# Encoder layer with retrieval FFN on one core: u blocks between the attention heads, unsplit first-pattern scores, and higher gather rates in the mixing and the up tiles

## The chip, the cores and the metric

The kernel runs on one core of a Trainium2 chip. The metric is the device time of one execution in microseconds (us), lower is better. The engines are named as in the profile: PE (TensorE; PEld is its weight load), DVE (VectorE), ACT (ScalarE), POOL (GpSimd), SP (SyncE, which issues the plain transfers).

## The reference, cut to what matters

One layer of an encoder with 512 tokens of width 1024, then a final norm.

```
h = rmsnorm(x); proj = h @ w_in            # u, v, q (3 patterns x 8 heads x 64), k, v, two gates
y_a = gelu(u) * spatial_gate(rmsnorm(gelu(v)))
y_b = softmax-merge over 3 patterns of banded ALiBi attention(q, k, v)
x = x + (sigmoid(ga) * (y_a @ wa) + sigmoid(gb) * (y_b @ wb)) @ wo
h = rmsnorm(x)
q = h @ w_q                                # 8 heads, two halves of 128
s = q . sub_keys; 16 best of each half; 16 best of the 256 sums -> 128 experts a token
a = gelu(u_tab[expert] . h) * softmax(best)
x = x + sum over experts of a * v_tab[expert]
out = rmsnorm(x)
```

The tables u_tab and v_tab hold 16,384 rows of 1024 floats each.

## The kernel before

**Tokens.** The 512 tokens are four tiles of 128, one for each residue modulo 4. Tile 0 goes ahead alone ("phase A": attention, gating, merge, residual, scores and routing in plain fp32). Tiles 1 to 3 follow together as a group of 384 columns ("phase B"), with fp32 operands split into a high and a low half of type fp32r (helper `split`: ACT makes the high half, DVE the low one) and three matmuls a product in `mm` (L114 to L116). Weights stream through `stream`: SP loads a block of 128 x 1024 floats (512 KB, tile `raw`, four buffers), the block is split into `whi` and `wlo` (two buffers each), and PE uses it. One such block is called a weight pair here, since it holds two slices of the contraction.

**Two ways through the experts.** Tiles 1 and 2 take the dense way: for each of 128 expert blocks an up tile `pu_t` (gelu(u h)) is multiplied by a gate matrix that is built from one-hot rows (`hot`, L760, in `gates`; matmul `pg`; kept in DRAM as `g_dram`, read back as `gl`), and 128 v tiles are accumulated in `acc`. The first 28 pairs of up tiles, 56 in all, are made ahead of the main loop in fp32 (`early`, L112); the other 72 in the main loop with split operands. Tiles 0 and 3 take the sparse way: each of their 128 experts a token is fetched by an indirect transfer of 128 rows, 512 KB, on POOL's queue (L239, `row_of`; eight buffers).

**Gather steps.** The sparse work is a generator, `all_steps`, of 517 steps. For tile 0: 128 u rows, each a dot product on DVE (L261), then 128 v rows in 32 groups of four. A group is eight PE matmuls of 32 columns into `acc_A` (L290): four rows by two halves, written as four different column blocks of the array one after the other, and each of them shows as two records in a trace. Then for tile 3: four routing steps on scores that come back from DRAM, its index tile `eidx` (L329), 128 u rows on DVE (L261) and 128 v rows, each a multiply-add on DVE (`xg`, L338). `gather_steps(us, behind)` is called behind each weight split (WUS), each attention head (HUS), each early up tile (PUS) and each tile of the main loop; it adds `us * rate` to what is owed and takes that many steps. The rate is MIX (0.55) from the attention to the scores of phase B, ATT (0.45) for heads, PRE (0.38) in the early up tiles, and in the main loop whatever spreads the steps that are left. The steps of a place are ordered behind the instructions named there; beyond that the tile scheduler puts the instructions of each engine in an order when the program is built, and each engine runs its own list in that order.

**Places that the change touches.** `attention` projects q in three blocks and runs four pairs of heads behind them; scores of the first pattern are split (`khl`, `q1`), those of the other two are plain fp32. `gating` then projects u in two blocks of four weight pairs, multiplies by the gate `z`, and splits the result into `yaT`. `merge`, `residual` and `scores` follow ("the mixing" below is everything from the merge to the scores of phase B).

## Time and profile before

| what | us |
|---|---|
| median of three runs (1831.03 to 1840.84) | 1839.69 |
| the profiled execution, its own time | 1839.34 |
| its span, first to last instruction | 1837.5 |
| PE busy | 1660.7 (90%) |
| DVE busy | 1324.8 (72%) |
| ACT busy | 715.3 (39%) |
| POOL busy | 696.7 (38%) |
| mean granted TensorE clock, share of full speed | 0.952 |

The transfers moved 548.5 MB, 299 GB/s over the span. A busy share over the whole span mixes stages with different limits, so the stages have to be read one by one. The profiled execution lies within 0.4 us of the median.

### The profile page before, as it was taken

The page shows a single profiled execution, that of the slowest core. Times are in us where ns is not written, and L with a number is a line of the kernel's source. Part 1 is how long each engine was busy: PE and PEld are TensorE (multiplying, and loading weights), DVE is VectorE, ACT ScalarE, POOL GpSimd, SP SyncE. Part 2 cuts the span into 40 slices and gives each one's busy share as a digit, 9 for nine tenths or more (in the row PEclk, how much of TensorE's full clock was granted, in tenths as well). Part 3 has the DMA queues.
Part 4 walks back from the last instruction along what each step waited for, and adds up shares of the span by engine and source line. Part 5 has one row for each costly group of instructions (what it writes and reads, how often), then busy time and mean ns, then how long its engine had stood idle before and what let it go on. Part 6 is the DMA issues. An engine that isn't in the chain of part 4 may idle for free.

```text
span 1837.5 us, 25573 instructions
## 1 busy us (share of the span) xinstructions
PE 1660.7 (90%) x9184; PEld 1390.9 (76%) x9184; DVE 1324.8 (72%) x2818; ACT 715.3 (39%) x1264; POOL 696.7 (38%) x535
## 2 busy tenths in 40 slices
PE   7999887999789999899999976687999999999997
PEld 6988866877589664787778965465768888878886
DVE  3332119899999233488976986598898998988896
ACT  4324211354433212233777830233444444444443
POOL 0000000378774443234431025465554554544440
PEclk9999998998799999899999997988999999999999
DMA  5234875599898888777787589999999999999994
GB/s 194 92 114 153 271 262 188 194 359 356 297 331 320 302 308 282 263 290 281 275 304 265 211 329 403 378 374 362 338 382 351 368 399 358 394 361 364 362 354 150
DMA packets 164335, 548.53 MB, mean 299 GB/s; under 512 B 17008, under 2 KB 37488, under 8 KB 163056
## 3 DMA queue, kind: packets, MB, share of 16 engines
q1 hardware_dynamic: 90480, 278.43, 42.5%
q0 software_dynamic: 73728, 268.47, 39.0%
q8 instruction: 72, 1.18, 0.2%
q14 instruction: 55, 0.45, 0.1%
HBM read 522.19 MB, written 24.64 MB: 298 GB/s over the span
## 4 chain that ended last, share of the span: by engine, by line
PE 61%; DVE 18%; DMA 10%; issue 6%; ACT 3%; POOL 1%; SPq 0%; DVEq 0%; POOLq 0%; ACTq 0%
PE pj L112 6%; PE pj L114 6%; PE pj L116 6%; PE pj L115 6%; PE acc L115 5%; PE pu_t L112 5%; PE acc L116 5%; DVE row L261 4%; PE acc L114 4%; PE acc_A L290 4%; PE pu_t L116 2%; DMA gl<-g_dram 2%; PE pu_t L114 2%; PE pu_t L115 2%; DVE vl L90 2%
## 5 line engine op out<-in xcount | busy, mean ns | idle before, releaser
L239 POOL DMA_INDIRECT row<-in_u_dram,eidx x256 | 363.1, 1418 | 298.5 <-DVE eidx L270 92.0
L261 DVE SCALAR_TENSOR_TENSOR row<-row,h2g 128x1024 f32<-128x1024 f32 x256 | 307.8, 1218 | 12.8 <-DMA row<-in_u_dram,eidx 12.7
L239 POOL DMA_INDIRECT row<-in_v_dram,eidx x128 | 182.0, 1422 | 182.8 <-DVE row L261 86.5
L239 POOL DMA_INDIRECT row<-in_v_dram,eT x128 | 141.7, 1107 | 250.3 <-PE acc_A L290 201.5
L112 PE MATMUL pu_t<-h2T,raw 128*128 128x256 f32 x896 | 209.5, 390 | 28.8 <-DMA raw<-in_ut_dram 28.8
L115 PE MATMUL acc<-vl,ah 128*128 128x512 f32 x512 | 207.2, 416 | 29.0 <-DVE vl L90 28.8
L90 DVE TENSOR_TENSOR wlo<-raw,whi 128x1024 fp32r<-128x1024 f32 x88 | 107.5, 1222 | 155.7 <-ACT whi L89 154.4
L112 PEld LDWEIGHTS pu_t<-h2T,raw 128*128 128x128 f32 x896 | 171.6, 196 | 62.7 <-issue 36.9
L114 PE MATMUL acc<-vh,ah 128*128 128x512 f32 x512 | 194.0, 412 | 17.4 <-ACT vh L89 13.0
L116 PE MATMUL acc<-vh,al 128*128 128x512 f32 x512 | 199.5, 408 | 0.0
L89 ACT CAST whi<-raw 128x1024 fp32r<-128x1024 f32 x88 | 92.3, 1048 | 267.6 <-PE pj L115 177.7
L90 DVE TENSOR_TENSOR vl<-raw,vh 128x1024 fp32r<-128x1024 f32 x128 | 156.1, 1222 | 32.0 <-ACT vh L89 31.9
L114 PE MATMUL pu_t<-h2S_hi,uhi 128*128 128x256 f32 x576 | 164.9, 286 | 6.1 <-ACT uhi L89 5.0
L116 PE MATMUL pu_t<-h2S_hi,ulo 128*128 128x256 f32 x576 | 164.5, 286 | 2.3 <-DVE ulo L90 2.3
L115 PE MATMUL pu_t<-h2S_lo,uhi 128*128 128x256 f32 x576 | 164.4, 285 | 0.0
L338 DVE SCALAR_TENSOR_TENSOR xg<-row,act,xg 128x1024 f32<-128x1024 f32 x128 | 163.9, 1281 | 0.4
L151 POOL TENSOR_TENSOR rs<-ms,mhalf 128x1 f32<-128x1 f32 x16 | 9.0, 563 | 400.5 <-DVE ms L149 302.0
L115 PEld LDWEIGHTS acc<-vl,ah 128*128 128x128 f32 x512 | 100.5, 196 | 65.6 <-DVE vl L90 44.5
L89 ACT CAST vh<-raw 128x1024 fp32r<-128x1024 f32 x128 | 133.0, 1044 | 24.2 <-DMA raw<-in_v_dram 20.1
L114 PEld LDWEIGHTS acc<-vh,ah 128*128 128x128 f32 x512 | 97.6, 197 | 45.3 <-ACT vh L89 19.4
L116 PE MATMUL pj<-hT_hi,wlo 128*128 128x384 f32 (+1 forms) x320 | 103.3, 359 | 18.7 <-DVE wlo L90 18.7
L114 PEld LDWEIGHTS pu_t<-h2S_hi,uhi 128*128 128x128 f32 x576 | 111.5, 194 | 10.8 <-ACT uhi L89 7.2
(238 smaller groups left out, 3426.3 us busy)
## 6 DMA issues: line engine op xcount, KB each, us to landing
raw<-in_ut_dram SPq DMA_DIRECT2D x128, 512.0 KB, 7.0
raw<-in_v_dram SPq DMA_DIRECT2D x128, 512.0 KB, 6.4
raw<-in_w_in_dram SPq DMA_DIRECT2D x88, 512.0 KB, 4.3
raw<-in_wq_dram SPq DMA_DIRECT2D x32, 512.0 KB, 4.5
g_dram<-stg SPq DMA_DIRECT2D x8, 2048.0 KB, 7.4
gl<-g_dram SPq DMA_DIRECT2D x32, 512.0 KB, 8.8
raw<-in_wa_dram SPq DMA_DIRECT2D x16, 512.0 KB, 5.6
raw<-in_wo_dram SPq DMA_DIRECT2D x16, 512.0 KB, 4.8
```

The costliest lines, as they stand in the source:

```text
L89: nc.scalar.copy(hi, src)
L90: return nc.vector.tensor_tensor(lo, src, hi.bitcast(F32), ALU.subtract)
L112: on_pe = nc.tensor.matmul(ps, l[0], r[0], start=first, stop=last)
L114: nc.tensor.matmul(ps, l[0], r[0], start=first, stop=False)
L115: nc.tensor.matmul(ps, l[0], r[1], start=False, stop=False)
L116: on_pe = nc.tensor.matmul(ps, l[1], r[0], start=False, stop=last)
L151: nc.gpsimd.tensor_tensor(rs, ms, mhalf, ALU.pow)
L239: nc.gpsimd.indirect_dma_start(out=row, out_offset=None, in_=table, in_offset=bass.IndirectOffsetOnAxis(ap=at, axis=0))
L261: nc.vector.scalar_tensor_tensor(row, row, 1.0, h2g, op0=ALU.mult, op1=ALU.mult, accum_out=ab[:, k:k + 1])
L290: nc.tensor.matmul(ps[32 * j:32 * j + 32, c], ex[:, j, :], rows[j][:, c], start=n == 0, stop=n == 31)
L338: nc.vector.scalar_tensor_tensor(xg, row, act[:, k:k + 1], xg, op0=ALU.mult, op1=ALU.add)
```

## The change

- The first pattern's scores are one plain fp32 matmul on `kk` and `q`; the split copies `khl` of k and the split of q go away, and k is copied out of PSUM by ACT instead of DVE.
- In phase B the two u blocks of `gating` are projected between the heads of the attention (hook `between`), kept in fp32 in `yaF`, and split into `yaT` after the attention.
- The first q projection of phase B gets a higher scheduling priority.
- Rates: a head takes 4.5 x 0.50 = 2.25 steps (2.03 before), a weight pair of the attention and of the u blocks 4.2 x 0.50 = 2.10 (2.31), a weight pair of the mixing 4.2 x 0.70 = 2.94 (2.31), an early up tile 4.5 x 0.45 = 2.03 (1.71).

```diff
--- before.py
+++ after.py
@@ -40,9 +40,9 @@
 GB = 16
 RB = 4
 GPB = 8
-MIX = 0.55
-ATT = 0.45
-PRE = 0.38
+ATT = 0.5
+MIX = 0.7
+PRE = 0.45
 WUS = 4.2
 HUS = 4.5
 PUS = 4.5
@@ -117,7 +117,7 @@
 
     steps = iter(())
 
-    rate = MIX
+    rate = ATT
     owed = 0.0
     taken = 0
 
@@ -419,7 +419,6 @@
         qsc = kv.tile([P, 4], F32, name="qsc")
         nc.sync.dma_start(qsc, a["qsc"])
         kk = kv.tile([P, 4, 512], F32, name="kk")
-        khl = Op(kv, [P, 4, 512], "khl", False)
         v_sb = kv.tile([P, NR, 512], F32, name="v_sb")
         z = zc.tile([P, NR, D], F32, name="z")
 
@@ -449,8 +448,7 @@
                 nc.vector.scalar_tensor_tensor(z[:, n, :], z[:, n, :], rs, gsgu, op0=ALU.mult, op1=ALU.mult)
 
             def ev_k(b, ps):
-                nc.vector.tensor_copy(kk[:, b, :], ps)
-                khl.put((slice(None), b), kk[:, b, :])
+                nc.scalar.copy(kk[:, b, :], ps)
 
             def ev_v(r, ps):
                 nc.scalar.copy(v_sb[:, r, :], ps)
@@ -465,7 +463,7 @@
                                         sgb[:, g, :].unsqueeze(1).to_broadcast([P, NR, P]), ALU.add)
 
 
-        def attention(pl, cl, x, ybT, exact, hook):
+        def attention(pl, cl, x, ybT, exact, hook, between=None):
             n = len(cl) * P
             bias = pl.tile([P, len(cl), 768], F32, name="bias", bufs=1)
             nc.sync.dma_start(bias, a["abias"][:, cl[0]:cl[-1] + 1, :])
@@ -473,11 +471,11 @@
 
             def q_of(hp):
                 if qs[hp] is None:
-                    qs[hp] = (Op(pl, [P, n], "q1", False), pl.tile([P, 2, n], F32, tag="q2", name="q2"))
+                    qs[hp] = pl.tile([P, 3, n], F32, tag="q", name="q")
                 return qs[hp]
 
             def heads(hp):
-                q1, q2 = q_of(hp)
+                q = q_of(hp)
                 po = pv.tile([P, 512], F32, tag="pv", name="po")
                 for j, r in enumerate(cl):
                     tok = slice(j * P, j * P + P)
@@ -486,9 +484,9 @@
                         slope = 2.0 ** -(head + 1)
                         rows = slice(64 * hh, 64 * hh + 64)
                         s = pst.tile([P, 1024], F32, tag="s", name="s")
-                        mm(s[:, 0:512], q1[rows, tok], khl[rows, hp, :], True, True)
+                        nc.tensor.matmul(s[:, 0:512], q[rows, 0, tok], kk[rows, hp, :], start=True, stop=True)
                         for g in range(2):
-                            nc.tensor.matmul(s[:, 512 + 128 * g:640 + 128 * g], q2[rows, g, tok],
+                            nc.tensor.matmul(s[:, 512 + 128 * g:640 + 128 * g], q[rows, 1 + g, tok],
                                              kk[rows, hp, r * P:(r + 1) * P], start=True, stop=True)
                         pr = pl.tile([P, 768], F32, tag="pr", name="pr", bufs=3)
                         mx = sp.tile([P, 1], F32, tag="mx", name="mx")
@@ -505,7 +503,7 @@
                             last = nc.vector.tensor_tensor(own, own, pr[:, 512 + 128 * g:640 + 128 * g], ALU.add)
                         nc.scalar.activation(pr[:, 0:512], pr[:, 0:512], AF.Copy, scale=rd)
                         if hook:
-                            gather_steps(HUS * ATT / MIX, last)
+                            gather_steps(HUS, last)
                         t = transpose4([pr[:, i * P:(i + 1) * P] for i in range(4)])
                         pt = pl.tile([P, 4, P], F32, tag="pt", name="pt")
                         nc.scalar.copy(pt, t)
@@ -517,32 +515,29 @@
             for j in range(3):
                 def ev_q(b, ps):
                     hp, g = divmod(4 * j + b, 3)
-                    q1, q2 = q_of(hp)
-                    sc = qsc[:, hp:hp + 1]
-                    if g:
-                        nc.scalar.activation(q2[:, g - 1, :], ps, AF.Copy, scale=sc)
-                    else:
-                        nc.scalar.activation(q1.t[0], ps, AF.Copy, scale=sc)
-                        nc.vector.scalar_tensor_tensor(q1.t[1], ps, sc, q1.t[0].bitcast(F32),
-                                                       op0=ALU.mult, op1=ALU.subtract)
-
-                proj_T(a["w_in"][4 + j], KT, x, n, ev_q, exact, hook)
+                    nc.scalar.activation(q_of(hp)[:, g, :], ps, AF.Copy, scale=qsc[:, hp:hp + 1])
+
+                with tc.high_priority(offset=0 if j or not hook else 250):
+                    proj_T(a["w_in"][4 + j], KT, x, n, ev_q, exact, hook)
                 heads(j)
+                if between:
+                    between(j)
             heads(3)
 
-        def gating(pl, cl, x, yaT, exact, hook):
+        def gating(pl, cl, x, put, c, exact, hook):
             n = len(cl) * P
-            for c in range(2):
-                def ev_u(b, ps):
-                    g = 4 * c + b
-                    u = pl.tile([P, n], F32, tag="u", name="u", bufs=3)
-                    nc.scalar.activation(u, ps, AF.Gelu)
-                    u4 = u.rearrange("p (r m n) -> p r n m", r=len(cl), n=NR)
-                    for j, r in enumerate(cl):
-                        nc.vector.tensor_tensor(u4[:, j], u4[:, j], z[:, :, g * P + 32 * r:g * P + 32 * r + 32], ALU.mult)
-                    yaT.put((slice(None), g), u)
-
-                proj_T(a["w_in"][7 + c], KT, x, n, ev_u, exact, hook)
+
+            def ev_u(b, ps):
+                g = 4 * c + b
+                u = pl.tile([P, n], F32, tag="u", name="u", bufs=3) if pl else yaF[:, g, :]
+                nc.scalar.activation(u, ps, AF.Gelu)
+                u4 = u.rearrange("p (r m n) -> p r n m", r=len(cl), n=NR)
+                for j, r in enumerate(cl):
+                    nc.vector.tensor_tensor(u4[:, j], u4[:, j], z[:, :, g * P + 32 * r:g * P + 32 * r + 32], ALU.mult)
+                if put:
+                    put(g, u)
+
+            proj_T(a["w_in"][7 + c], KT, x, n, ev_u, exact, hook)
 
         def merge(pl, cl, x, yaT, ybT, mT, exact, hook):
             n = len(cl) * P
@@ -611,7 +606,8 @@
             with ExitStack() as gq:
                 attention(pool(gq, "qA", 2), [0], lambda kt: hA[:, kt, :], ybT, True, 0)
             m_ = pool(ga, "mA", 1, reuse_waits="tile")
-            gating(m_, [0], lambda kt: hA[:, kt, :], yaT, True, 0)
+            for c in range(2):
+                gating(m_, [0], lambda kt: hA[:, kt, :], lambda g, u: yaT.put((slice(None), g), u), c, True, 0)
             mT = Op(ya_, [P, KT, P], "mA", True)
             merge(m_, [0], lambda kt: hA[:, kt, :], yaT, ybT, mT, True, 0)
             h2A = Op(ya_, [P, KT, P], "h2A", True)
@@ -645,15 +641,23 @@
         py = ExitStack()
         y_ = pool(py, "yB", side="right", reuse_waits="tile")
         ybT = Op(y_, [P, 4, NG], "ybB", False)
+        yaF = y_.tile([P, KT, NG], F32, name="yaF")
         with ExitStack() as gq:
-            attention(pool(gq, "qB", 2, reuse_waits="tile"), GROUP, hB, ybT, False, WUS)
+            qb = pool(gq, "qB", 2, reuse_waits="tile")
+
+            def ev_block(c):
+                if c < 2:
+                    gating(None, GROUP, hB, None, c, False, WUS)
+
+            attention(qb, GROUP, hB, ybT, False, WUS, ev_block)
         pat.close()
+        rate = MIX
         pva = ExitStack()
         acc_A.append(pool(pva, "pva", 1, side="right", space=PSUM, reuse_waits="tile").tile([P, D], F32, name="acc_A"))
         yaT = Op(pool(py, "yaB", side="right", reuse_waits="tile"), [P, KT, NG], "yaB", False)
-        with pz:
-            with ExitStack() as gu:
-                gating(pool(gu, "uB", reuse_waits="tile"), GROUP, hB, yaT, False, WUS)
+        pz.close()
+        for g in range(KT):
+            yaT.put((slice(None), g), yaF[:, g, :])
         pk.close()
         with ExitStack() as gm:
             mT = Op(pool(gm, "mTB", reuse_waits="tile"), [P, KT, NG], "mB", False)
```

The scheduler's order moves with it. The first place is PE in the scores of phase B: `pj` are the products of the scores' projection, `ps` the scores of one block, `acc_A` the matmuls of tile 0's v rows; the number behind x counts matmuls in a row. Before:

```order
L116 MATMUL pj<-h2B_hi,wlo 128x384
L290 MATMUL acc_A<-row,ex 32x512 x8
L603 MATMUL ps<-skc,qT 128x128 x12
L114 MATMUL pj<-h2B_hi,whi 128x384
L115 MATMUL pj<-h2B_lo,whi 128x384
L116 MATMUL pj<-h2B_hi,wlo 128x384
L114 MATMUL pj<-h2B_hi,whi 128x384
```

After the change, at the same place:

```order
L290 MATMUL acc_A<-row,ex 32x512
L114 MATMUL pj<-h2B_hi,whi 128x384
L115 MATMUL pj<-h2B_lo,whi 128x384
L116 MATMUL pj<-h2B_hi,wlo 128x384
L114 MATMUL pj<-h2B_hi,whi 128x384
L115 MATMUL pj<-h2B_lo,whi 128x384
L116 MATMUL pj<-h2B_hi,wlo 128x384
L290 MATMUL acc_A<-row,ex 32x512 x6
L598 MATMUL ps<-skc,qT 128x128 x9
L290 MATMUL acc_A<-row,ex 32x512
L598 MATMUL ps<-skc,qT 128x128 x3
```

The eight matmuls of a group stood together here before; now a group comes as five and three single ones with `pj` or `ps` between them. Over the whole mixing PE's list has 160 matmuls of `acc_A` in 42 runs before (10 of them of eight, 9 of five, 17 of one) and 192 in 89 runs now (20 of five, 65 of one).

The second place is DVE where the early up tiles give way to the main loop: `eidx` are the indices of tile 3, `row,ab` its u rows, `hot` the one-hot rows of the dense gates, `pre` the early up tiles that are multiplied by the gates. Before, from `eidx` on:

```order
L90 TENSOR_TENSOR h2S_lo<-h2T,h2S_hi 128x2048
L329 CAST eidx<-ef_g 128x128
L234 SCALAR_TENSOR_TENSOR o<-xg,rs,gfin 128x512 x2
L841 TENSOR_TENSOR pre<-pre,gl 128x256 x8
L90 TENSOR_TENSOR al<-pre,ah 128x256 x2
L841 TENSOR_TENSOR pre<-pre,gl 128x256 x8
L261 SCALAR_TENSOR_TENSOR row,ab<-row,h2g 128x1024 x6
L841 TENSOR_TENSOR pre<-pre,gl 128x256 x8
L261 SCALAR_TENSOR_TENSOR row,ab<-row,h2g 128x1024
L841 TENSOR_TENSOR pre<-pre,gl 128x256 x8
L261 SCALAR_TENSOR_TENSOR row,ab<-row,h2g 128x1024 x7
L841 TENSOR_TENSOR pre<-pre,gl 128x256 x8
```

After the change:

```order
L234 SCALAR_TENSOR_TENSOR o<-xg,rs,gfin 128x512 x2
L329 CAST eidx<-ef_g 128x128
L764 TENSOR_TENSOR hot<-iota,tt 128x1024 x4
L261 SCALAR_TENSOR_TENSOR row,ab<-row,h2g 128x1024 x3
L764 TENSOR_TENSOR hot<-iota,tt 128x1024 x2
L261 SCALAR_TENSOR_TENSOR row,ab<-row,h2g 128x1024 x3
L764 TENSOR_TENSOR hot<-iota,tt 128x1024 x2
L261 SCALAR_TENSOR_TENSOR row,ab<-row,h2g 128x1024 x4
L764 TENSOR_TENSOR hot<-iota,tt 128x1024 x2
```

All 64 `hot` stood ahead of `eidx` before. Now the last 32 stand behind it and take turns with the u rows of tile 3.

The third place is PE in the early up tiles (`pu_t`, eight matmuls a tile) behind the transposes `tr` for the second token tile's gates, with `pg` for the one-hot matmuls. Before:

```order
L750 MATMUL tr<-ident,ijf 128x128 x2
L750 MATMUL tr<-ident,g_5541 128x128
L112 MATMUL pu_t<-h2T,raw 128x256 x4
L290 MATMUL acc_A<-row,ex 32x512 x8
L112 MATMUL pu_t<-h2T,raw 128x256 x8
L768 MATMUL pg<-hot 128x128 x8
L112 MATMUL pu_t<-h2T,raw 128x256 x9
L768 MATMUL pg<-hot 128x128 x8
```

After the change:

```order
L754 MATMUL tr<-ident,ijf 128x128 x2
L112 MATMUL pu_t<-h2T,raw 128x256 x10
L754 MATMUL tr<-ident,g_5540 128x128
L112 MATMUL pu_t<-h2T,raw 128x256 x13
L772 MATMUL pg<-hot 128x128 x8
L112 MATMUL pu_t<-h2T,raw 128x256 x9
L772 MATMUL pg<-hot 128x128 x8
```

The rows of `acc_A` are no longer in this stretch, since the last group now stands ahead of it (12 early up tiles are behind PE when the last group comes, 25 before). The first eight `pg` of the second token tile, which need the first of the 32 `hot` that moved, stand behind 26 early up tiles.

## Rows read from the trace of the kernel before

**Rows 1.** The page, part 1: busy us (share of the span), instructions.

```profile
PE 1660.7 (90%) x9184; PEld 1390.9 (76%) x9184; DVE 1324.8 (72%) x2818; ACT 715.3 (39%) x1264; POOL 696.7 (38%) x535
```

**Rows 2.** Windows, stage by stage, all engines.

```profile
core 0: us, PE busy (x) PEld busy (x) DVE busy (x) ACT busy (x) POOL busy (x), PEclk, DMA share, GB/s
354.00:590.00 236.00, 208.16 (x1081) 183.66 (x1080) 226.87 (x462) 99.69 (x157) 175.45 (x125) 0.88 0.93 342
590.00:842.00 252.00, 241.89 (x1294) 175.95 (x1294) 115.41 (x314) 67.47 (x96) 94.78 (x91) 0.98 0.80 286
842.00:1079.00 237.00, 237.00 (x1404) 194.28 (x1403) 204.72 (x728) 166.34 (x383) 49.16 (x41) 1.00 0.72 261
1079.00:1169.00 90.00, 56.81 (x213) 45.10 (x213) 48.51 (x101) 6.78 (x18) 41.56 (x35) 0.85 1.04 404
1169.00:1376.00 207.00, 176.96 (x666) 132.01 (x665) 187.67 (x249) 77.77 (x115) 121.48 (x82) 0.92 0.97 363
1376.00:1826.00 450.00, 425.28 (x2603) 375.79 (x2602) 394.37 (x507) 195.39 (x298) 203.18 (x141) 0.98 0.94 353
```

**Rows 3.** Timeline of DVE at the stage ends (start us, us, instruction).

```profile
590.12 0.28 DVE L275 TENSOR_TENSOR act<-act,gate 128x128 f32<-128x128 f32 x1
...
1079.24 0.22 DVE L329 CAST eidx<-ef_g 128x128 int32<-128x128 f32 x1
...
1169.19 1.22 DVE L90 TENSOR_TENSOR vl<-raw,vh 128x1024 fp32r<-128x1024 f32 x1 [16.32 <-ACT vh L89]
...
1374.57 1.21 DVE L90 TENSOR_TENSOR vl<-raw,vh 128x1024 fp32r<-128x1024 f32 x1
1375.71 1.21 DVE L90 TENSOR_TENSOR ulo<-raw,uhi 128x1024 fp32r<-128x1024 f32 x1
```

**Rows 4.** The chain that ended last, 842 to 874 us (start us, us).

```profile
842.34 3.46 PE pu_t L112 x16
845.80 1.85 PE acc_A L290 x16
...
871.71 1.78 PE pg L768 x16
```

**Rows 5.** Windows, the matmuls of `acc_A` alone (line L290).

```profile
590.00:842.00 252.00, 61.66 (x320) 11.19 (x320) 0.98 0.80 286
842.00:1079.00 237.00, 28.08 (x192) 5.69 (x192) 1.00 0.72 261
```

**Rows 6.** Timeline of PE in the merge: a short and a whole run.

```profile
630.34 0.34 PE L115 MATMUL pj<-hT_lo,whi 128*128 128x384 f32 x1
630.61 1.05 PE L290 MATMUL acc_A<-row,ex 128*32 128x512 f32 x2
631.58 0.44 PE L116 MATMUL pj<-hT_hi,wlo 128*128 128x384 f32 x1
631.86 0.34 PE L114 MATMUL pj<-hT_hi,whi 128*128 128x384 f32 x1
632.04 0.33 PE L115 MATMUL pj<-hT_lo,whi 128*128 128x384 f32 x1
...
662.33 1.93 PE L290 MATMUL acc_A<-row,ex 128*32 128x512 f32 x16
664.18 0.44 PE L114 MATMUL pj<-ybB_hi,whi 128*128 128x384 f32 x1
```

**Rows 7.** Windows, `hot` alone (line L760).

```profile
842.00:1079.00 237.00, 74.99 (x64) 1.00 0.72 261
```

**Rows 8.** Timeline of PE in the main loop.

```profile
1405.65 0.40 PE L114 MATMUL acc<-vh,ah 128*128 128x512 f32 x1
1405.88 0.40 PE L115 MATMUL acc<-vl,ah 128*128 128x512 f32 x1
...
1406.35 0.28 PE L114 MATMUL pu_t<-h2S_hi,uhi 128*128 128x256 f32 x1
1406.47 0.28 PE L115 MATMUL pu_t<-h2S_lo,uhi 128*128 128x256 f32 x1
```

## The prediction

> **What bounds the kernel now.** I read the windows first, cut where the work changes hands [rows 2]; the cuts come from the timeline of DVE [rows 3] and from the chain that ended last [rows 4]. Read in each row which engine leaves no time over.
>
> From 354 to 590 us (attention and u blocks of phase B, with tile 0's u rows) DVE is busy for 226.9 of 236 us: DVE is the bound. From 590 to 842 (the mixing) PE is busy for 241.9 of 252 and DVE for less than half: PE is the bound, and what is added to PE's list there is paid in full. From 842 to 1079 (56 early up tiles) PE shows 237 of 237, but what ends the stretch is DVE, which has 204.7 us of routing and `hot` in its list ahead of `eidx`, and about 32 us of waits; until `eidx` is there, no row of tile 3 can be fetched, and transfers fill only 0.72 of their time. From 1079 to 1169 PE, DVE and ACT all have room, and the transfers stand at a share of 1.04 and 404 GB/s: transfers are the bound. From 1169 to 1376 (v tiles alone) DVE has 187.7 of 207 and transfers a share of 0.97: these two share the bound. From 1376 to 1826 (up and v tiles) all three are close: PE 425, DVE 394, transfers 0.94 of 450. The page's 90% for PE [rows 1] hides all this.
>
> **What the change does, in order of time.** The prices come from one execution, and the sum is made against it: its own time is 1839.34 us, span 1837.5, which is the median of the runs shown within 0.4 us.
>
> *Ahead of 354 us.* The split of k and of tile 0's q goes away, k's copy goes to ACT, and eight unsplit scores come in. An fp32 up tile of 256 columns takes 3.46 us for 16 records [rows 4], 0.22 a record and two records a matmul, so 512 columns are about 0.86 us; three split matmuls of 512 columns stand 0.23 apart [rows 8], 0.70 together. So a head costs 0.16 us more on PE, 1.3 us for tile 0's eight heads, and some of it is hidden. I take 0, bounds -5 and +3.
>
> *To 590 us.* In phase B the same 0.16 us for 24 heads is 4 us on PE, which has 28 us to spare in this stretch, so it is hidden behind DVE; if DVE were not the bound it would cost these 4 us. The u blocks bring PE work into a stretch that has room for it, but no DVE work goes away by moving: by DVE's list up to the last u row, three more weight splits stand ahead of it (1.14 us each, the distance of two operations in [rows 3]), eight small operations of the merge come with them, and four splits of q are gone. That is about +5 us, against 9 us of DVE's idle time that better filled lists may win back. I take +3, bounds -6 and +5: the last u row at 593.
>
> *The mixing, now 252 us.* The three weight pairs done early come off PE: 24 matmuls at 0.18 us [rows 6] each, 4.3 a pair, -13. Now the v rows of tile 0. By rates, 24 groups fall here instead of 20. But the price of a group hangs on how its eight matmuls stand. A whole run of eight (16 records) takes 1.85 us [rows 4, 6], so its matmuls, of four column blocks, overlap; a single matmul (2 records) takes 0.97 us, because it has nothing beside it, and on both sides the neighbouring products stand 0.27 and 0.28 apart instead of 0.18, so that it costs 1.16 us in all; a whole run costs 2.03 with the same 0.19 for its neighbours. The order shows 17 single matmuls and 25 longer runs before, 65 and 24 now. With longer runs at the price of a whole one that is 17 x 1.16 + 25 x 2.03 = 70 us before (61.7 busy [rows 5], and 42 x 0.19 for the neighbours: 70), and 65 x 1.16 + 24 x 2.03 = 124 now: +54 us on the engine that is the bound. Lower bound: the mean price of a group before, 70 / 20 = 3.5, for four groups more, +14; upper bound +58, with the shorter runs of before at less. I take 54, since the list of PE is fixed and the rows are of the same kind. The mixing is then 252 - 13 + 54 = 293 us and ends at 886. Transfers have room for 16 more rows here (0.80).
>
> *The early up tiles to `eidx`, now 237 us.* Half of the `hot` now stand behind `eidx`: 32 x 1.17 us [rows 7] = -37. Of DVE's 32 us of waits I take back 19, as an estimate: the last v rows of tile 0 now end with the 12th early tile instead of the 25th, but no row here says how many of the waits hang on them; bounds 0 and 28. That leaves 181 us: `eidx` at 1067, 12 us sooner than now. PE will not fill this stretch any more: 26 up tiles at 3.46 are 90 us, 128 `pg` of two records at 0.11 [rows 4] are 28, and the v rows left, 64 matmuls in 13 single and 10 longer runs, 35; so it comes to the first `pg` that needs a moved `hot` at about 1039 and waits there for some 30 us. This wait is new. Behind it in PE's list stand 30 early up tiles, behind those SP's loads (four `raw` buffers), so the loads of 26 up tiles are left undone in a time when transfers have room.
>
> *From `eidx` to the first v tile, now 90 us at 404 GB/s, 36 MB.* Into this stretch the change pulls: 75 rows of tile 3 that stand in DVE's list ahead of the first v tile (31 before), with eight more in the buffers 43.5 MB at 512 KB each; 26 up tiles, 13.6 MB; the four gate blocks of the second token tile, written at 2.1 MB each, 8.4; 14 loads of `gl`, 7.3; spilled up tiles, `x1` and the first v tiles, 6. Together 79 MB; at 404 GB/s that is 196 us. DVE alone has some 147 us of work for it (32 `hot`, 75 rows, 40 small products), and PE 30 up tiles and 128 `pg`, 132 us. I take 196, since the nearest row is a stretch with the same kinds of transfers; bounds 147 and, at the 363 GB/s of the next stage, 218. The first v tile comes at 1263.
>
> The Trainium skill, "DMA: Bandwidth & Descriptors", section Specifications, gives about 358 GB/s as a core's limit from HBM. The trace disagrees with 404 GB/s over 90 us; by the page's figure the stretch would be 221 us and the time 25 us above mine, and I hold to the row.
>
> *v tiles alone, now 207 us.* 71 rows instead of 82 stand among the 56 tiles in DVE's list: -11 x 1.14 = -13, 194 us, to 1457.
>
> *Up and v tiles, now 450 us.* 110 rows instead of 147: DVE loses 42 us of work and the transfers 19 MB, so both fall clear of the bound. PE's own work is 72 x (24 x 0.12 + 12 x 0.23) = 406 us [rows 8]. I take 418, bounds 406 and 450. This is the change's gain, 32 us; the end of the loop is at 1875. The tail of 11.5 us and the 1.8 us around the span stay: **1889 us**.
>
> So 48 rows leave the last two stages and give 45 us back there; but 44 of them are moved no further than to the stretch behind `eidx`, which the transfers bound and which grows by 106, while the stretch ahead of it gives 56; and the mixing pays 41 for the broken runs less the pairs done early. Sum: 3 + 41 - 56 + 106 - 13 - 32 = +49.
>
> **Rivals.** *No change (1843 us):* the single matmuls cost no more than a group did, +8 us for four whole runs instead of +54. For it: the runs of before are broken too, and PE held. Against it: the pieces stand in the trace with 0.97 us each, and PE had 10 us free in 252. Chance 0.12.
>
> *Faster (about 1798 us):* the rows between the `hot` are hidden, because the stretch from the end of the mixing to the first v tile is paced by PE and not by `eidx` and transfers. PE's work there is 56 x 3.46 for the up tiles, 57 for 256 `pg` and 35 for the v rows left, 286 us; then the first v tile is at 886 + 286 = 1172, 91 us sooner than I have it. For it: transfers have room up to `eidx` (0.72). Against: rows can't be fetched ahead of `eidx`, and 79 MB have to pass behind it. It wins where this stretch takes no more than its present 327 us; I have 377. Chance 0.16.
>
> *Slower still (1911 to 1921 us):* either the transfers behind `eidx` move at 363 GB/s, +22, or the last stage stays at 450 us, +32, because PE waits for v and up tiles and not for rows. For it: in the last stage 44 us of PE's time over its own work are not put down to rows alone by any view. Against: with 37 rows fewer, both DVE and transfers have 10% to spare. Chance 0.14.
>
> **How the numbers follow.** My forecast, 1889 us and 1855 to 1910 by its own bounds, has a chance of 0.58. Within 0.5% (1830 to 1849, about what a measurement can tell from no change) lies the first rival with a little of the forecast's lower edge, 0.13; faster by more is the second rival, 0.16; slower is the rest, 0.71. The range reaches down to the first rival and up to the last one: 1843 to 1921. Left out are the faster case and a few of the rest.
>
> **What would show it.** The mixing of the changed kernel takes some 293 us, and `acc_A` (L290) is busy there for about 110 us with 384 records. `eidx` comes near 1067 and PE has a hole of about 30 us ahead of it. From there to the first v tile the transfers stand at a share near 1 for 190 us or more. In the last stage PE is busy for 97% and the transfers for 0.88. If the mixing takes 250 to 260 us, the step on broken runs is wrong; if the first v tile is there within 327 us of the mixing's end, the step on transfers behind `eidx` is wrong, and the kernel is faster or unchanged; if the last stage keeps 450 us, the rows were not what bound it.

## The result and the profile after

The changed kernel takes 1906.76 us (median of 4 runs, 1903.46 to 1909.41) against 1836.74 us for the kernel before in the same comparison: a ratio of 1.0383, 95% interval 1.0346 to 1.0419, so 3.8% slower. The forecast was 1889 us, range 1843 to 1921. The profiled execution has a span of 1904.4 us and is the one read here.

The page's busy line of the changed kernel, to be held against [rows 1]:

```profile
PE 1709.7 (90%) x9152; PEld 1376.1 (72%) x9152; DVE 1321.2 (69%) x2802; ACT 718.5 (38%) x1267; POOL 709.2 (37%) x535
```

DVE has no more work than before, and the bytes are the same 548.5 MB; PE has 49 us more with 32 instructions fewer. More time in fewer instructions is the first sign that something got dearer, not more.

The windows by stage of the changed kernel, cut at the same events as [rows 2]:

```profile
356.00:606.00 250.00, 226.55 (x1147) 191.65 (x1145) 233.24 (x468) 105.84 (x167) 169.38 (x124) 0.88 0.91 328
606.00:898.00 292.00, 282.99 (x1270) 163.54 (x1270) 111.14 (x315) 62.83 (x89) 109.48 (x104) 0.99 0.76 262
898.00:1079.00 181.00, 147.66 (x780) 107.58 (x778) 165.20 (x687) 88.90 (x199) 29.93 (x29) 0.91 0.58 211
1079.00:1275.00 196.00, 154.16 (x771) 132.86 (x771) 143.40 (x201) 83.98 (x200) 115.42 (x81) 0.90 1.00 387
1275.00:1470.00 195.00, 167.59 (x663) 124.95 (x662) 174.94 (x234) 76.85 (x113) 109.86 (x74) 0.95 0.97 372
1470.00:1893.00 423.00, 414.26 (x2607) 372.15 (x2605) 352.56 (x453) 196.62 (x298) 163.99 (x104) 1.00 0.90 330
```

Stage by stage: the attention 250 us (236 before), the mixing 292 (252), the early up tiles 181 (237), the stretch behind the indices 196 (90), the v tiles alone 195 (207), the last stage 423 (450). The second stage has fewer matmuls than before (1270 records for 1294) and takes 41 us more of PE.

The windows of the matmuls of `acc_A` alone, on PE, in the mixing and in the early up tiles ([rows 5] before: 61.66 us and 28.08 us):

```profile
606.00:898.00 292.00, 115.19 (x384) 0.99 0.76 262
898.00:1079.00 181.00, 31.11 (x131) 0.91 0.58 211
```

Over both stages the work is the same 256 matmuls, and it costs 146 us instead of 90. Why is seen in PE's timeline of the changed kernel, in the merge:

```profile
642.13 0.33 PE L116 MATMUL pj<-yaB_hi,wlo 128*128 128x384 f32 x1
642.39 1.05 PE L290 MATMUL acc_A<-row,ex 128*32 128x512 f32 x2
643.37 0.44 PE L114 MATMUL pj<-yaB_hi,whi 128*128 128x384 f32 x1
643.65 0.34 PE L115 MATMUL pj<-yaB_lo,whi 128*128 128x384 f32 x1
...
649.25 1.90 PE L290 MATMUL acc_A<-row,ex 128*32 128x512 f32 x10
651.08 0.44 PE L116 MATMUL pj<-yaB_hi,wlo 128*128 128x384 f32 x1
```

A single matmul holds PE for 0.98 us (642.39 to 643.37). Five in a row hold it for 1.83 us (649.25 to 651.08), as long as all eight do [rows 6]. So a group that comes as five and three single ones pays for the five what the whole group would cost, and then three times nearly 1 us more.

Waits in PE's timeline and in the table of waits belong to the later stages. In the early up tiles, from PE's timeline:

```profile
1039.55 0.38 PE L754 MATMUL tr<-ident,ijf 128*128 128x128 f32 x2
1039.77 4.48 PE L112 MATMUL pu_t<-h2T,raw 128*128 128x256 f32 x20
1077.59 0.47 PE L754 MATMUL tr<-ident,g 128*128 128x128 f32 x1 [33.34 <-DVE g L219]
```

PE stands for 33 us in front of the transpose of `g`, the gate of the second dense tile. The routing of that tile is done by then: DVE runs the first operation of its gate at 1016.8 us, but the last one (L219) only at 1077.2, because the routing of tile 3 now stands between them in DVE's list; before the change they ran at 936.6 and 942.1. `eidx` follows at 1078.8 and the first of the moved `hot` at 1078.9. The first `pg` that needs one of those runs at 1085.3 and does not wait for it.

In the stretch behind `eidx` (1079 to 1275; engine, line, what it waited for, us in total, times, longest):

```profile
POOL row L239 <- DVE row L261: 36.9, 11, 17.3
...
PE pu_t L112 <- DMA raw<-in_ut_dram: 30.2, 6, 12.7
DVE pre L845 <- DMA gl<-g_dram: 23.5, 3, 12.6
```

Here PE and DVE both wait for transfers, at a DMA share of 1.00.

### The profile page after: what moved, and what is told of

It is laid out like the page before. It is cut to its first block, busy times and chain, and to the rows that moved or that the text cites. A ratio compares the mean times of both kernels' runs of the same rounds, so it can differ in the third digit from the quotient of the medians.

```text
span 1904.4 us, 25506 instructions
## 1 busy us (share of the span) xinstructions
PE 1709.7 (90%) x9152; PEld 1376.1 (72%) x9152; DVE 1321.2 (69%) x2802; ACT 718.5 (38%) x1267; POOL 709.2 (37%) x535
## 4 chain that ended last, share of the span: by engine, by line
PE 71%; DVE 12%; DMA 9%; issue 4%; ACT 3%; POOL 1%; SPq 1%; DVEq 0%; POOLq 0%; ACTq 0%
PE acc_A L290 7%; PE pj L116 7%; PE pj L114 7%; PE pu_t L112 6%; PE pj L115 6%; PE pj L112 6%; PE acc L115 5%; PE acc L116 5%; PE acc L114 5%; DVE row L261 4%; PE pu_t L116 3%; PE pu_t L114 3%; PE pu_t L115 3%; PE pg L772 2%; DMA raw<-in_v_dram 2%
## 5 line engine op out<-in xcount | busy, mean ns | idle before, releaser
L239 POOL DMA_INDIRECT row<-in_u_dram,eidx x256 | 367.4, 1435 | 329.4 <-DVE row L261 109.0
L239 POOL DMA_INDIRECT row<-in_v_dram,eidx x128 | 195.0, 1524 | 208.4 <-DVE xg L338 111.9
L112 PE MATMUL pu_t<-h2T,raw 128*128 128x256 f32 x896 | 216.6, 396 | 34.0 <-DMA raw<-in_ut_dram 30.2
L239 POOL DMA_INDIRECT row<-in_v_dram,eT x128 | 137.0, 1070 | 240.0 <-PE acc_A L290 186.5
L116 PE MATMUL acc<-vh,al 128*128 128x512 f32 x512 | 193.0, 399 | 0.0
L290 PE MATMUL acc_A<-row,ex 128*32 128x512 f32 x512 | 146.3, 612 | 0.0
L114 PE MATMUL pj<-hT_hi,whi 128*128 128x384 f32 (+1 forms) x320 | 114.6, 359 | 8.4 <-ACT sig L550 7.9
```

The lines of the kernel that those rows point to most:

```text
L112: on_pe = nc.tensor.matmul(ps, l[0], r[0], start=first, stop=last)
L114: nc.tensor.matmul(ps, l[0], r[0], start=first, stop=False)
L116: on_pe = nc.tensor.matmul(ps, l[1], r[0], start=False, stop=last)
L239: nc.gpsimd.indirect_dma_start(out=row, out_offset=None, in_=table, in_offset=bass.IndirectOffsetOnAxis(ap=at, axis=0))
L290: nc.tensor.matmul(ps[32 * j:32 * j + 32, c], ex[:, j, :], rows[j][:, c], start=n == 0, stop=n == 31)
```

## The experiments

All ratios are to the kernel before, measured on the same chip in the same comparison. "Price" below is the prediction's: 1.16 us for a single `acc_A` matmul and 2.03 for a longer run, counted in PE's list of the mixing.

**Whole runs, in the changed kernel and in the one before.** One line of `down`, in each of the two kernels: the row that lands last is multiplied first. The first matmul of a group then has to wait for the last row, and once it is placed, the other seven are ready; PE's list has 22 runs of eight in the mixing of the changed kernel instead of 89 pieces, and 20 instead of 42 in that of the kernel before.

```diff
-                for j in range(4):
+                for j in (3, 0, 1, 2):
                     c = slice(f * 512, f * 512 + 512)
```

> The changed kernel with one line different: the eight matmuls of a group of v rows begin with the row that lands last, so that the scheduler leaves them together. PE's list then has 176 of them in 22 runs of eight in the mixing (192 in 89 runs in the changed kernel); the rows of tile 3 and the one-hot work stand as in the changed kernel. Theory of the broken runs (a whole run 2.03 us, a single matmul 1.16): the mixing falls from 292 us by 79 to some 213 us, up to 235 if its transfers then hold it; the stages behind it keep their lengths, and the span falls from 1904 to 1825 to 1847. Rival 'number': the rows themselves, their transfers and DVE work, cost the time, not how the matmuls stand; then the mixing stays at 280 to 292 and the span above 1890. Rival 'structure': u blocks and unsplit scores cost it; then the span stays within 1% of 1904.

> The kernel of before with the same one line: 20 whole runs in the mixing instead of 42 pieces, all else in the order as before. Theory of the broken runs: the mixing falls from 252 by 30 us to some 222, the rest follows, span 1800 to 1815. Rivals 'number' and 'structure': within 0.5% of before.

Measured: the changed kernel with whole runs takes 1823.88 us, ratio 0.9966 (0.9939 to 0.9994), span 1818.3, which is 7 us below its expectation; the kernel before with whole runs takes 1814.75 us, ratio 0.9897 (0.9864 to 0.993), span 1814.8, at the upper end of its expectation. The windows of the mixing of the changed kernel with whole runs, all engines, and of `acc_A`'s matmuls there, on PE:

```profile
599.00:817.00 218.00, 206.76 (x1237) 160.46 (x1238) 109.27 (x305) 62.05 (x88) 97.65 (x97) 0.97 0.91 334
```

```profile
599.00:817.00 218.00, 43.54 (x352) 0.97 0.91 334
```

22 groups of eight matmuls cost 43.5 us; 24 cost 115.2 when broken. The mixing falls from 292 to 218 us, 74 of the 86 us by which the span falls. So the broken runs are the loss, and some of it was there before the change already: 25 us by the mixing of the kernel before, 252 us against 227 with whole runs. With whole runs in both kernels the change costs 4 us of span (1818.3 against 1814.8); with broken ones it costs 67 (1904.4 against 1837.5).

**Old rates, and new rates alone.** The first is the changed kernel with the steps per place as they were; the second the kernel before with the new rates and nothing else.

```diff
-ATT = 0.5
-MIX = 0.7
-PRE = 0.45
+ATT = 0.55
+MIX = 0.55
+PRE = 0.38
...
-                            gather_steps(HUS, last)
+                            gather_steps(HUS * 0.45 / 0.55, last)
```

> The changed kernel with the rates of before at every place, so that u blocks and unsplit scores alone are left of the change. The order then has 160 matmuls of v rows in 57 runs in the mixing (42 before, 89 in the changed kernel), no one-hot operation behind the indices, and 147 rows in the last stage. Theory: the attention stays 14 us longer, the mixing takes 252 - 13 + 15 = 254 us, all stages behind it are as before (237, 90, 207, 450); span some 1855, 1% over before and 2.6% under the changed kernel. Rival 'structure': the span stays within 1% of 1904. Rival 'number': 1837 to 1851, with a mixing of 239.

> The kernel before with the new rates alone; its attention, split scores and u blocks stay as they were. More v rows of tile 0 fall into the mixing by this than in the changed kernel: 232 matmuls of acc_A in 110 runs, 79 of them single ones, 155 us by the prices of the prediction against 70 before; half of the one-hot work stands behind the indices of tile 3, and 74, 77 and 105 rows in the last three stages. Theory (broken runs, then transfers behind the indices): attention and mixing together grow from 488 to 572 us, so the first early up tile is at 926; the stretch from the indices to the first v tile takes 196 us; the span is 1915 to 1950, longer than the changed kernel's, and the rates alone make the loss. Rival: a group costs what it did on the average before (3.5 us); then the first early up tile is at 874 and the span is 1865 to 1890.

Measured: with old rates 1848.1 us, ratio 1.0102 (1.0058 to 1.0146); the mixing takes 251 us, and the stretch behind `eidx` 90 us as before the change. The span of 1844.8 us is 10 us under the one expected and lies in the range of the rival 'number', but the mixing is the theory's (254 expected) and not that rival's (239). With new rates alone 1939.05 us, ratio 1.0592 (1.0544 to 1.064), span 1939.2, slower than the changed kernel itself. Two stages of the kernel with new rates alone, mixing and the stretch behind `eidx`, and `acc_A` in that mixing:

```profile
582.00:937.00 355.00, 348.08 (x1550) 202.48 (x1548) 130.73 (x341) 74.59 (x104) 122.62 (x123) 0.99 0.74 257
...
1107.00:1304.00 197.00, 155.15 (x775) 132.81 (x774) 142.94 (x202) 83.48 (x201) 113.86 (x82) 0.89 1.00 386
```

```profile
582.00:937.00 355.00, 141.90 (x464) 0.99 0.74 257
```

The first early up tile came at 937.5 us, where the theory of broken runs had 926 and the mean price of a group 874. The rates make the loss. With them, the rest of the change takes part of it back (24 groups stand in the mixing against 29 here, and three weight pairs fewer); without them, it costs 1.0%, and the attention is the only stage that is longer than before (250 us against 236).

**The one-hot work first.** The changed kernel, with no step of tile 3 taken until the one-hot products of both dense tiles are written:

```diff
+    cap = 257
...
-            while owed >= 1:
+            while owed >= 1 and taken < cap:
...
+    cap = 9999
     for n in range(G0, npre):
```

> The changed kernel with the routing of tile 3 held back until the one-hot work of the dense gates is in the program: 10 instead of 32 of the one-hot operations stand behind the indices of tile 3, 51 instead of 75 rows stand between the indices and the first v tile, 95 instead of 71 among the v tiles, 110 in the last stage as now; the mixing is as in the changed kernel. Theory of the transfers behind the indices: indices some 26 us later (1105), the stretch behind them some 141 us instead of 196, first v tile near 1246, but the stage of v tiles alone 27 us longer (222), so that the last stage begins near 1468 as now; span 1890 to 1904. Rival 'wait': PE's wait for the moved one-hot operations is what costs; with it gone the span falls by 30 us to some 1870.

Measured: 1896.45 us, ratio 1.0367 (1.0324 to 1.041), span 1893.1. Windows of the early up tiles and of the stretch behind `eidx`:

```profile
899.00:1102.00 203.00, 202.46 (x1104) 157.75 (x1105) 188.71 (x706) 134.13 (x310) 29.85 (x29) 1.00 0.65 235
1102.00:1237.00 135.00, 95.88 (x450) 79.25 (x448) 89.87 (x143) 39.53 (x90) 72.44 (x56) 0.86 1.03 404
```

PE's hole of 33 us is gone (202 of 203 us busy; DVE has finished the gate `g` at 1026.5 us), and the stretch behind `eidx` is 62 us shorter; but `eidx` comes 24 us later, and the v tiles alone take 30 us more. 11 us stay. What was taken out of the transfers' stretch came back next to it.

**Half the bytes of tile 3's rows.** The changed kernel, with each of these rows fetched at half width and used twice by DVE; it leaves half of the columns of tile 3's u and v rows out.

```diff
-            row = row_of(a["u"], eidx[:, k0 + k:k0 + k + 1])
+            row = row_of(a["u"], eidx[:, k0 + k:k0 + k + 1], half)
...
-                row = row_of(a["v"], eidx[:, k0 + k:k0 + k + 1])
+                row = row_of(a["v"], eidx[:, k0 + k:k0 + k + 1], D // 2)
```

> The changed kernel with every gathered u and v row of tile 3 fetched at half its width, 256 KB instead of 512 KB; DVE's work on them is unchanged, and the order too but for small shifts (88, 57 and 111 rows in the stretch behind eidx, in that of the v tiles alone and in the last). It leaves half of the columns of tile 3's u and v rows out. Theory: transfers bound the stretch from eidx to the first v tile. It then moves some 57 MB instead of 79, 141 us at 404 GB/s, and DVE's own work (143 us in the changed kernel, 13 more rows of 1.14) comes to 158: so DVE takes over and the stretch is 155 to 172 us instead of 197 in spite of 13 more rows; the stretch of v tiles alone is 160 to 180 instead of 195. Rival: the stretch is long because DVE, PE and POOL wait for each other and not for bytes; then it stays at 196 us or, with 13 more rows, 211.

Measured: 1863.89 us, ratio 1.0175 (1.0132 to 1.0217), 40 us below the changed kernel's span at 1864.7. The stretch behind `eidx` in it:

```profile
1079.50:1256.40 176.90, 154.48 (x777) 132.46 (x775) 155.72 (x215) 84.97 (x201) 136.54 (x93) 0.94 0.90 325
```

57.5 MB (325 GB/s over 176.9 us) instead of 75.9, and 177 us instead of 196 with 13 rows more of DVE's work: transfers bounded it, for these 20 us at least. The size was missed by 5 us, since DVE, which should have become the bound with 158 us, is busy for 156 of 177 and still waits 20 us for rows. The v tiles alone fell from 195 to 180 us, the last stage, whose bound is PE, by 5.

**What makes the attention longer.** Three parts of the change, each tried by itself: the u blocks put behind the heads in the changed kernel, and the unsplit scores, or the priority of the first q block, put into the kernel before.

```diff
-            attention(qb, GROUP, hB, ybT, False, WUS, ev_block)
+            attention(qb, GROUP, hB, ybT, False, WUS)
+            for c in range(2):
+                ev_block(c)
```

```diff
-                        mm(s[:, 0:512], q1[rows, tok], khl[rows, hp, :], True, True)
+                        nc.tensor.matmul(s[:, 0:512], q[rows, 0, tok], kk[rows, hp, :], start=True, stop=True)
```

```diff
-                proj_T(a["w_in"][4 + j], KT, x, n, ev_q, exact, hook)
+                with tc.high_priority(offset=0 if j or not hook else 250):
+                    proj_T(a["w_in"][4 + j], KT, x, n, ev_q, exact, hook)
```

> The changed kernel with the two u blocks behind the last pair of heads instead of between the heads; rates, unsplit scores and priority stay. The list of the mixing stays broken: 186 matmuls of acc_A in 87 runs, 124 us by the prices of the prediction, as in the changed kernel. Theory: the u blocks between the heads are what made the attention (first to last u row of tile 0) 250 us long instead of 236, by waits of DVE on splits of ACT. Then it is 236 to 242 us here, and DVE's wait of 9.1 us on whi at the weight split goes back to some 2 us; the mixing gets three weight pairs back (+13, 300 to 306 us), so the span is 1895 to 1910. Rival: unsplit scores or the priority of the first q block made it long; then the attention stays at 247 to 252 us with the wait of 9 us, and the span is 1908 to 1920.

> The kernel before with the unsplit scores of the first pattern alone (k copied by ACT, no split of k and q, one plain fp32 matmul). In the mixing 160 matmuls of acc_A stand in 47 runs (42 before), 75 us by the prices of the prediction (70). Theory: unsplit scores cost PE 4 us in the attention, hidden behind DVE, so the attention is 236 to 243 us, the mixing 252 to 258, and the span 1836 to 1850. Rival: ACT's copies of k and the plain matmuls are what lengthened the attention; then it is 247 to 252 us, with a wait of DVE on whi of 9 us, and the span is 1848 to 1860.

> The kernel before with the higher priority of the first q projection alone. Theory: the priority is what is left of the edits as a cause of the longer attention; then it takes 247 to 252 us (first to last u row of tile 0) with 13 us of idle DVE or more. Rival: the three more weight pairs and the merge's small products in DVE's list, 7 us of work, and an idle time that differs by up to 7 us from run to run are all there is; then it takes 236 to 244. In both cases the rest is as before and the span is 1830 to 1855.

Measured: u blocks behind the heads 1913.59 us, ratio 1.0447 (1.0392 to 1.0502); unsplit scores alone 1832.8 us, ratio 1.0001 (0.9976 to 1.0026); priority alone 1829.98 us, ratio 1.0008 (0.998 to 1.0035). The windows of the attention in these three, in this order:

```profile
356.50:608.70 252.20, 219.04 (x1147) 188.23 (x1145) 234.36 (x467) 109.31 (x168) 171.55 (x124) 0.90 0.89 326
```

```profile
354.00:591.00 237.00, 208.81 (x1066) 177.53 (x1065) 226.11 (x458) 98.56 (x156) 173.60 (x124) 0.90 0.91 339
```

```profile
352.00:588.00 236.00, 204.47 (x1078) 180.86 (x1077) 226.79 (x459) 99.01 (x157) 171.72 (x124) 0.89 0.93 341
```

The theory on the u blocks falls: without them between the heads the attention is as long as in the changed kernel, although DVE's wait for `whi`, which it rested on, fell from 9.1 us to 2.7. The rows of both waits, of the changed kernel and of the one with the u blocks behind the heads:

```profile
DVE wlo L90 <- ACT whi L89: 9.1, 8, 1.7
```

```profile
DVE wlo L90 <- ACT whi L89: 2.7, 5, 0.9
```

The mixing of that kernel did not get three weight pairs back either: it takes 290 us where 300 to 306 were expected, since 30 weight splits still stand ahead of the last u row. Unsplit scores and priority cost nothing either; both spans (1825.3 and 1828.3 us) came out below the expected ranges. The seven kernels that keep u in `yaF` and split it later all have 6 to 8 us more of DVE's work ahead of the last u row than the kernel before (30 weight splits instead of 27, small products of the merge), and 14 to 19 us of idle DVE. Of the seven that split u at once (27 splits in five of them, and 22 and 25 in the two whose rates bring the last u row sooner), six have 9 to 11 us idle and one 16; with whole runs alone, where nothing in the attention is changed, it is the 16. The work is settled. The idle part is not: `yaF` by itself was not tried.

**Better versions.** Three combinations: the changed kernel with whole runs, one-hot work first and u blocks behind the heads; the kernel before with whole runs and unsplit scores; the kernel before with whole runs, one-hot work first and a rate of 0.62 in the mixing (the line of `down` and the cap as above, and this):

```diff
         pat.close()
+        rate = 0.62
         pva = ExitStack()
```

> The changed kernel with three edits together: a group's last row is multiplied first (whole runs of eight matmuls), no step of tile 3 goes out ahead of the one-hot work of the dense gates, and the u blocks stand behind the heads. Effects seen in single runs are added up: from the changed kernel 1904, whole runs -86, one-hot work first -11, u blocks behind the heads between -10 and +10: a span of 1797 to 1817, ahead of the kernel before with whole runs (1814.8) or level with it. Rival: with the mixing short, the rows of tile 3 that the one-hot work displaces come back in the last two stages: 1818 to 1830.

> The kernel before with unsplit scores of the first pattern and a group's last row multiplied first. In the mixing 160 matmuls of acc_A stand in 20 whole runs of eight, 41 us by the prices of the prediction against 75 in 47 runs. Theory: the gain of whole runs adds to the unsplit scores, which cost nothing by themselves: mixing 222 to 230 us, span 1805 to 1822. Rival: the mixing is held up by weight loads and not by acc_A once the scores change; then it stays at 250 us and the span is 1830 to 1845.

> The kernel before with whole runs, a rate of 0.62 instead of 0.55 in the mixing, and no step of tile 3 ahead of the one-hot work of the dense gates. Five more groups in the mixing, all whole: 25 runs, 51 us against 41 at the old rate; 51, 71 and 134 rows in the last three stages against 26, 83 and 147. Theory: the mixing takes 237 us, the early up tiles 220 (5 groups fewer and ten one-hot products behind the indices), the stretch behind the indices 135 to 145, the v tiles alone 190, the last stage 437 to 442: the bytes that leave the last stage come back in the stretch ahead of it, so the span is 1805 to 1822, level with whole runs alone. Rival: the early up tiles are bound by PE and shrink by more, and the span is 1790 to 1805.

Measured: 1812.26 us, ratio 0.9887 (0.9844 to 0.9931); 1807.82 us, ratio 0.988 (0.9843 to 0.9917); 1799.65 us, ratio 0.9837 (0.9799 to 0.9876). The first two have spans inside their expectations (1813.9 and 1807.3 us). The last is the fastest kernel of the study, but its interval overlaps the others', and that of the kernel before with whole runs alone; which part of its gain is the rate's and which that of the one-hot work put first was not tried apart. It came out below its expectation, as its rival had it: the early up tiles, of which this is the window, are bound by PE and take 192 us where 220 were expected.

```profile
832.00:1024.00 192.00, 191.04 (x1116) 159.81 (x1114) 189.19 (x714) 135.90 (x320) 25.88 (x23) 1.00 0.66 236
```

## Why the prediction was right, by its own steps

The direction and the two mechanisms that carry the loss, broken runs and transfers behind `eidx`, were right, and of the 18 us by which the median lies above the forecast 16 are in two terms, the attention and the last stage.

| term of the sum | forecast, us | changed kernel, us |
|---|---|---|
| attention (first to last u row) | 239 | 250.2 |
| mixing | 293 | 292.1 |
| early up tiles to `eidx` | 181 | 180.7 |
| `eidx` to the first v tile | 196 | 196.6 |
| v tiles alone | 194 | 195.0 |
| up and v tiles | 418 | 422.8 |

*The attention* is the step that was mis-sized: +14 us instead of +3. Its work was close (+5 forecast; DVE's busy time grew by 6.4, from 226.87 to 233.24). Wrong was to let better filled lists win back 2 us of idle time: it grew from 9 to 17, and the term lies beyond its own bound of +5. A list that holds more kinds of work was taken to wait less, with no row that said so.

*The broken runs* were the largest unknown and came out within 1 us, with the work the step named: 115 us of `acc_A` for a forecast of about 110. The price holds from 20 runs in the mixing to 110, within 6 us where the mixing is taken alone and within 13 where the attention is taken with it. In the table, "forecast" is 252 us plus the difference of the prices, less 13 us for the three weight pairs in the kernels that keep u in `yaF`; for the rates alone and the rate of 0.62, where the last u row moves too, attention and mixing are taken together.

| kernel | runs in the mixing | price, us | forecast, us | measured, us |
|---|---|---|---|---|
| changed, whole runs | 22 | 45 | 213 | 218.2 |
| before, whole runs | 20 | 41 | 222 | 227.3 |
| before, unsplit scores | 47 | 75 | 257 | 255.5 |
| changed, old rates | 57 | 85 | 254 | 251.3 |
| changed | 89 | 124 | 293 | 292.1 |
| before, rate 0.62, whole runs (with attention) | 25 | 51 | 468 | 478.3 |
| before, new rates (with attention) | 110 | 155 | 572 | 584.4 |

The single matmul's price is confirmed from both sides: singles taken away (by whole runs) give the time back, and more of them (by rates alone) cost more. The kernels not listed lie within 6 us of the price's forecast; with whole runs the mixing is always 4 to 10 us longer than it.

The Trainium skill, "TensorEngine Tiling (Array Packing)", section Key Properties, says that different tiles of the array execute in parallel and that a change of the tiling mode drains the engine. The rows are in line with both: eight matmuls over four column blocks take 1.85 us and a single one 0.98, and the products on both sides stand 0.26 and 0.28 us from their next instead of 0.18. That a drain is what these neighbours wait for is not shown.

*PE's new wait* was forecast at some 30 us from about 1039 on; it is 33 us from 1044, but not where the step had it. PE stands in front of the transpose of the gate `g` and not in front of a `pg`, and waits for a last operation of the gate that fell behind tile 3's routing, not for a moved `hot`. The size came out because `g`, `eidx` and the first moved `hot` follow each other within 2 us on DVE. *Behind `eidx`*, 196 us came from two errors that cancel, which is luck: 75.9 MB and not 79, at 387 GB/s and not 404. That bytes bound the stretch is shown by the half rows; that what leaves it comes back next to it, by the one-hot work put first. *The last two stages* gave 39 us where 45 were forecast, and PE is the bound at the end (414 of 423 us), as the step said.

*The rivals.* "No change" falls with the mixing: 292 us with broken runs and 218 with whole ones. "Faster" falls too: the stretch from the mixing's end to the first v tile took 377 us, as forecast, and not 327, and it is shorter with half rows (358). The slower one needed 363 GB/s behind `eidx` or a last stage of 450 us; it had 387, and 423.

## What to carry to other kernels

Where several small matmuls share the array by column blocks, their price depends on standing together in PE's list: count runs there, not matmuls. Make the first of them the one whose operand lands last, so that a scheduler can't place some early; here this one line gave more than the whole change moved. A higher rate of background steps has to be priced where the steps land, at the price that they have in the foreground engine's list there: with broken runs the new rates cost 5.9%; with whole runs, the one-hot work first and a rate of 0.62 in the mixing the kernel is 1.6% faster than before, of which whole runs alone give 1.0%. That the rate gives the rest is not shown.

And a wait that shrinks is no proof of a cause: DVE's wait for ACT's splits fell by 6 us and the stage kept its length.

## What the runs showed of the hardware beyond that

Five `acc_A` matmuls in a row took as long as eight, 1.83 us against 1.85. Transfers ran at 404 GB/s for 135 us where the one-hot work came first, and at 386 to 387 for 196 us where it stood among the rows, both at a DMA share of 1.00 or more; what makes this difference was not tried.
